# Every other weight chunk of the mixer split by a casting and an adding DMA, the chunks between on VectorE

## The chip, the cores and the metric

The kernel runs on one core of a Trainium2 chip. The metric is the device time of one execution in microseconds; of several runs the median is given.

## What is computed

One layer of a decoder with hybrid attention over 16 meta tokens and 512 tokens, model width 1024, all in float32. Of the reference, cut:

```python
h = concat(meta_tokens, x)
u = rmsnorm(h, attn_norm)
z = u @ w_in                # q, k, v of three attentions, an indexer, three gates
y_sb = stick_breaking(q_sb, k_sb, v_sb)                  # 4 heads
y_sp = indexed_sparse_attention(rmsnorm(q_sp), rmsnorm(k_sp), v_sp,
                                q_ix, k_ix, w_ix, rel_bias, top_k)   # 4 heads
y_df = rmsnorm(differential_attention(...))              # 4 heads of two maps
merged = (sigmoid(g_sb + b) * (y_sb @ w_br_sb) + sigmoid(g_sp + b) * (y_sp @ w_br_sp)
          + sigmoid(g_df + b) * (y_df @ w_br_df))
h = h + merged @ w_out
zf = rmsnorm(h, ffn_norm) @ w_up
h = h + (silu(causal_conv3(gate half of zf)) * (value half of zf)) @ w_down
return h[16:]
```

## The kernel before

All weights lie in memory as 133 chunks of 128x1024 float32 (512 KB), each eight 128x128 blocks. A float32 product is made of three passes of TensorE in a reduced type, fp32r: each operand is split into a high part (its value rounded to fp32r) and a low part (what is left), and `mm3` (L311) runs over the chunk's blocks three times: high part of the weights with the high part of the activations, high with low, low with high. So the low part `wl` of a chunk is first read in the third pass of its first half of the tokens (258 or 264 columns), after 16 matmuls of the chunk, and last in the third pass of its second half.

The chunks are used one after the other in the order of the list `order` (L279). First come the indexer's three, then those that PLAN (L46) names: units (`sb`, `sp`, `df`: three chunks each, q, k and v of two heads or one differential pair), gates (`g`: four chunks for half of a branch's gate) and branches (`b`: the output projection of an attention, half of it), then W_OUT, W_UP and W_DN, the last two being the feed-forward part. While dense chunks run on TensorE, the attentions of the units before run as streams: generators that `tick` moves on, one step after every eight matmuls of a chunk. They advance by clocks that the kernel books for each engine (`book`, L87); what a stream does next, and in which order the engines get the work, hangs on these booked costs.

A chunk is prepared by `prep` (L299): its raw float32 lands in a buffer `wr` by a DMA from SP's queue (L296), ACT casts it into `wh`, and `sub` (L108) subtracts, wl = wr - wh, on GpSimd (G, the profile's POOL) or VectorE (V, DVE), whichever would end earlier by the booked clocks (with 1 us in favour of GpSimd). There are three raw buffers, two of wh and two of wl. Each user of a chunk k (`dense`, `branch`, `up` and the like) calls `prep(k)` and `prep(after.get(k))`, so the next chunk is prepared while this one is multiplied, and its raw data is loaded another chunk ahead. A wl buffer is free once TensorE has ended the third pass of the chunk two before.

Names that come up below: `xh`, `xl` are the activations' parts, `psd` and `psw` the PSUM banks of dense chunks and of streams, `tmp` work tiles of the streams, `r` a reciprocal of a softmax sum, `m` and `work` the top-k search, `G` gates, `y` an attention's output, `pm` and `pt` transposed weights of attention, `qk` queries and keys, moved between partitions by DMAs of SP's queue (L632), `W` a bias tile that a DMA from POOL's queue (L122, `gdma`) loads. Operations that go through the booking helper all have line 99.

The low part is chosen and written here:

```python
    def sub(out, a, b, hv=HV):
        t = clock["P"]
        tv = max(clock["V"], t) + V.cost(out) + hv
        e = G if max(clock["G"], t) + G.cost(out) < tv else V
        e.tensor_tensor(out, a, b, OP.subtract)
```

Of the kernel before, what the change touches and what calls it, by code (L numbers as in the profile page):

```python
# [8 lines left out]
F32 = mybir.dt.float32  # L9
F32R = mybir.dt.float32r  # L10
AF = mybir.ActivationFunctionType
OP = mybir.AluOpType
# [3 lines left out]
P = 128  # L16
# [24 lines left out]
W_BR, W_OUT, W_UP, W_DN = 51, 59, 67, 111  # L41
# [14 lines left out]
def tile_kernel(ctx: ExitStack, tc, hT, wpk, par, bias, yT):  # L56
    nc = tc.nc
# [16 lines left out]
    HVW = 1000  # L74
    HV = 500

    def book(e, cost):
        c = cur[0]
        clock[e] = max(clock[e], clock["P"]) + cost
        c["t"] = max(clock[e], c["t"] + cost, clock["P"] + cost) + LAT  # L80

    class Timed:
# [11 lines left out]
        def __getattr__(self, op):  # L94
            f = getattr(self.eng, op)

            def run(out, *a, **k):
# [5 lines left out]
    V = Timed("V", nc.vector, 1.04, 150, scalar_tensor_tensor=(1.25, 105), tensor_tensor_scan=(2.16, 110),  # L103
              tensor_tensor_reduce=(1.0, 255), match_replace=(1.04, 220))
    S = Timed("S", nc.scalar, 0.84, 190)
    G = Timed("G", nc.gpsimd, 2.3, 200)
# [7 lines that stand above are left out]
# [6 lines left out]
    def gdma(out, x):  # L120
        book("G", 1050)
        nc.gpsimd.dma_start(out, x)  # L122
# [9 lines left out]
    wp = ctx.enter_context(tc.tile_pool(name="wp", bufs=2))  # L132
# [43 lines left out]
    def tmp(dt=F32):  # L176
        return ap_.tile([P, T], dt, tag="tmp", bufs=caps["tmp"], name="tmp")
# [99 lines left out]
    wraw, wsp = {}, {}  # L277
    plan = PLAN.split()
    order = [W_IX, W_QIX, W_QIX + 1]  # L279
# [10 lines left out]
    assert sorted(order) == list(range(NCHUNK))  # L290
    after = dict(zip(order, order[1:]))

    def load(k):
        if k is not None and k not in wraw:
            r = wp.tile([P, 8, P], F32, tag="raw", bufs=3, name=f"wr{k}")
            nc.sync.dma_start(r, wpk[k].rearrange("p (j c) -> p j c", c=P))  # L296
            wraw[k] = r

    def prep(k):  # L299
        if k is None or k in wsp:  # L300
            return
        load(k)
        r = wraw[k]
        wh = wp.tile([P, 8, P], F32R, tag="wh", bufs=2, name=f"wh{k}")
        wl = wp.tile([P, 8, P], F32R, tag="wl", bufs=2, name=f"wl{k}")
        S.copy(wh, r)
        sub(wl, r, wh, HVW)
        wsp[k] = (wh, wl)
        load(after.get(after.get(k)))

    def mm3(out, prs, xh, xl, start=True, stop=True):  # L311

# [19 lines left out]
    rs = const.tile([P, T], F32, name="rs")  # L332
    take("tmp", 10)
    for k in (W_IX, W_QIX):
        wraw[k] = wp.tile([P, 8, P], F32, tag="raw", bufs=3, name=f"wr{k}")
        wsp[k] = tuple(wp.tile([P, 8, P], F32R, tag=t, bufs=2, name=f"{t}{k}") for t in ("wh", "wl"))
    hs = [tmp() for _ in range(KT)]

    def load_h(*kts):
# [16 lines left out]
    nc.sync.dma_start(prm[:, C_QSP:], par[:, C_QSP:])  # L356
    load_h(6, 7)
    load(order[2])

    def wbank():  # L360
# [115 lines left out]
    def dense(k, evac, halves=HALQ, q0=Q0, into=(psd, psd)):  # L476
        prep(k)
        prep(after.get(k))
        for hf, (o, n) in enumerate(halves):
            d = into[hf]()  # L480
            s0 = q0 + o
            mm3(d[:, :n], [(k, j, j) for j in range(KT)], lambda kt: xh[:, kt, s0:s0 + n],
                lambda kt: xl[:, kt, s0:s0 + n])
            with tc.high_priority(offset=PRI):
                evac(hf, o, n, d[:, :n])
# [39 lines left out]
    for g in range(2):  # L525
        qh = tmp(F32R)
        ql = tmp(F32R)

        def ev_qix(hf, o, n, d):
            raw = tmp()  # L530
            V.tensor_tensor(raw[:, :n], d, rs[:, Q0 + o:Q0 + o + n], OP.mult)
            S.copy(qh[:, o:o + n], raw[:, :n])
            V.tensor_tensor(ql[:, o:o + n], raw[:, :n], qh[:, o:o + n], OP.subtract)

        if g:
            dense(W_QIX + g, ev_qix, into=(psd, wbank))
        else:
            prep(W_QIX + 1)
            for hf, (o, n) in enumerate(HALQ):
                ev_qix(hf, o, n, qixd[hf][:, :n])  # L540

        qd = [dram.tile([P, TQ], F32, name=f"qd{g}{e}") for e in range(2)]
        for d, x in zip(qd, (qh, ql)):
            nc.sync.dma_start(d, x[:, :TQ].bitcast(F32))
        for r, d in ((0, qd[0]), (32, qd[1]), (64, qd[0])):
            nc.sync.dma_start(qst[g][r:r + 32].bitcast(F32), d.rearrange("(j p) t -> p j t", p=32))
# [514 lines left out]
    for m in range(8):  # L1061
        a = gates[0, m // 4][:, m % 4]
# [12 lines left out]
    def ft(dt=F32):  # L1075
        return ffn.tile([P, TQ], dt, tag="ft", bufs=10, name="ft")

    for m in range(8):
        nc.sync.dma_start(hm[:, m], hT[:, m, Q0:])
        k = W_OUT + m  # L1080
# [53 lines left out]
    for f in range(NF):  # L1134
# [6 lines left out]
        c = ft()  # L1141
# [4 lines left out]
        a = ft()  # L1146
# [9 lines left out]
    for m in range(8):  # L1156
# [3 lines left out]
        for c in sorted({e // 8 for e in range(e0, e1)}):  # L1160
            k = W_DN + c
# [82 lines left out]
```

## Time and profile before

| | before |
|---|---|
| runs, us | 912.95, 916.18, 915.88 |
| median, us | 915.88 |
| profiled execution, us (its span) | 913.53 (911.6) |
| granted TensorE clock, mean | 0.99 |
| PE busy in the span | 873.7 us, 96% |
| DVE busy | 554.9 us, 61% |
| ACT busy | 452.9 us, 50% |
| POOL busy | 322.3 us, 35% |
| DMA from SP's queue / from POOL's | 91.30 MB / 2.42 MB |

The profile is of one execution. The span is the time from its first to its last instruction; the execution's own time lies 1.9 us above it. Busy shares are means over the whole span: the mixer lasts to about 487 us, W_OUT to about 535, the feed-forward part the rest.

### The profile page before, as it was taken

The page shows a single profiled execution, that of the slowest core. Times are in us where ns is not written, and L with a number is a line of the kernel's source. Part 1 is how long each engine was busy: PE and PEld are TensorE (multiplying, and loading weights), DVE is VectorE, ACT ScalarE, POOL GpSimd, SP SyncE. Part 2 cuts the span into 40 slices and gives each one's busy share as a digit, 9 for nine tenths or more (in the row PEclk, how much of TensorE's full clock was granted, in tenths as well). Part 3 has the DMA queues.
Part 4 walks back from the last instruction along what each step waited for, and adds up shares of the span by engine and source line. Part 5 has one row for each costly group of instructions (what it writes and reads, how often), then busy time and mean ns, then how long its engine had stood idle before and what let it go on. Part 6 is the DMA issues. An engine that isn't in the chain of part 4 may idle for free.

```text
span 911.6 us, 15425 instructions
## 1 busy us (share of the span) xinstructions
PE 873.7 (96%) x6066; PEld 810.0 (89%) x6066; DVE 554.9 (61%) x1125; ACT 452.9 (50%) x848; POOL 322.3 (35%) x195
## 2 busy tenths in 40 slices
PE   7998999898999999889998999999999999999998
PEld 6988989798999999779998999999999999888886
DVE  6579988877677888787437445555555555322221
ACT  7466877676756686735654343333333333211110
POOL 2534233332445425665353233344444344200100
PEclk9999999999999999999999999999999999999999
DMA  6585213441234522432233433232333332233330
GB/s 231 163 247 177 70 47 104 107 118 47 71 98 118 139 67 87 106 92 68 70 93 118 137 91 95 93 93 93 93 93 93 93 93 93 93 117 105 116 101 23
DMA packets 32359, 94.68 MB, mean 104 GB/s; under 512 B 4313, under 2 KB 4457, under 8 KB 32288
## 3 DMA queue, kind: packets, MB, share of 16 engines
q1 hardware_dynamic: 31568, 91.30, 33.8%
q0 software_dynamic: 720, 2.42, 1.0%
q8 instruction: 47, 0.77, 0.4%
q14 instruction: 24, 0.20, 0.1%
HBM read 80.88 MB, written 5.86 MB: 95 GB/s over the span
## 4 chain that ended last, share of the span: by engine, by line
PE 71%; DVE 15%; ACT 8%; issue 3%; DMA 2%; POOL 1%; SPq 0%; DVEq 0%; ACTq 0%; POOLq 0%
PE psd L183 49%; PE psw L183 21%; DVE tmp L99 7%; ACT tmp L99 3%; DVE work L99 3%; DVE m L99 1%; PE psw L187 1%; DVE G L99 1%; ACT wh L99 1%; DMA qk<-qk 1%; ACT G L99 1%; DMA tmp<-hT 1%; POOL wl L99 1%; DVE pt L99 1%; DVE r L99 1%
## 5 line engine op out<-in xcount | busy, mean ns | idle before, releaser
L99 POOL TENSOR_TENSOR wl<-wr,wh 128x1024 fp32r<-128x1024 f32 x79 | 193.0, 2443 | 333.1 <-ACT wh L99 241.0
L99 ACT CAST wh<-wr 128x1024 fp32r<-128x1024 f32 (+2 forms) x137 | 139.4, 1020 | 175.4 <-PE psd L183 117.6
L183 PE MATMUL psd<-xh,wh 128*128 128x258 f32 (+2 forms) x792 | 118.4, 289 | 1.8 <-DVE tmp L99 1.2
L183 PE MATMUL psd<-xl,wh 128*128 128x258 f32 (+2 forms) x792 | 119.0, 290 | 0.0
L183 PE MATMUL psd<-xh,wl 128*128 128x258 f32 (+2 forms) x792 | 117.9, 289 | 0.0
L99 DVE TENSOR_TENSOR wl<-wr,wh 128x1024 fp32r<-128x1024 f32 (+3 forms) x58 | 67.0, 1157 | 69.0 <-PE psd L183 60.6
L183 PEld LDWEIGHTS psd<-xh,wh 128*128 128x128 f32 x792 | 104.5, 191 | 3.4 <-ACT kst L99 1.0
L183 PEld LDWEIGHTS psd<-xl,wh 128*128 128x128 f32 x792 | 104.9, 191 | 1.0
L183 PEld LDWEIGHTS psd<-xh,wl 128*128 128x128 f32 x792 | 104.8, 191 | 0.7
L99 ACT ACTIVATE tmp<-tmp 128x264 f32<-128x264 f32 (+7 forms) x154 | 69.2, 474 | 16.8 <-DVE tmp L99 14.5
L99 POOL TENSOR_TENSOR ft<-ft 128x512 f32<-128x512 f32 x22 | 46.5, 2114 | 82.5 <-DVE ft L99 79.1
L99 DVE SCALAR_TENSOR_TENSOR ft<-ft,prm 128x512 f32<-128x512 f32 x44 | 58.4, 1328 | 20.4 <-ACT ft L99 19.6
L183 PE MATMUL psw<-uh,wh 128*128 128x256 f32 (+2 forms) x264 | 47.0, 320 | 0.0
L183 PE MATMUL psd<-ul,wh 128*128 128x258 f32 (+2 forms) x264 | 46.9, 319 | 0.0
L183 PE MATMUL psw<-ul,wh 128*128 128x256 f32 (+2 forms) x264 | 46.9, 319 | 0.0
L183 PE MATMUL psd<-uh,wl 128*128 128x258 f32 (+2 forms) x264 | 46.8, 319 | 0.0
L183 PE MATMUL psw<-uh,wl 128*128 128x256 f32 (+2 forms) x264 | 46.8, 319 | 0.0
L183 PE MATMUL psd<-uh,wh 128*128 128x258 f32 (+2 forms) x264 | 46.8, 319 | 0.0
L183 PE MATMUL psd<-ah,wl 128*128 128x512 f32 x176 | 45.8, 396 | 0.0
L183 PE MATMUL psd<-al,wh 128*128 128x512 f32 x176 | 45.8, 396 | 0.0
L183 PE MATMUL psd<-ah,wh 128*128 128x512 f32 x176 | 45.8, 396 | 0.0
L99 ACT CAST ah<-ft 128x512 fp32r<-128x512 f32 x22 | 13.7, 622 | 64.6 <-POOL ft L99 64.6
(193 smaller groups left out, 1653.7 us busy)
## 6 DMA issues: line engine op xcount, KB each, us to landing
wr<-wpk SPq DMA_DIRECT2D x131, 512.0 KB, 3.6
qk<-qk SPq DMA_DIRECT2D x48, 132.0 KB, 3.7
gd<-tab SPq DMA_DIRECT2D x8, 328.0 KB, 6.2
tmp<-hT SPq DMA_DIRECT2D x8, 264.0 KB, 5.9
W<-gd POOLq DMA_DIRECT2D x8, 264.0 KB, 3.6
qk<-tmp SPq DMA_DIRECT2D x16, 128.5 KB, 2.3
hm<-hT SPq DMA_DIRECT2D x8, 257.0 KB, 4.3
yT<-ft SPq DMA_DIRECT2D x8, 256.0 KB, 2.0
```

Source lines behind the costliest of these rows:

```text
L99: return f(out, *a, **k)
L183: PE.matmul(out, lhsT, rhs, **k)
L187: PE.transpose(out, x, ident[:x.shape[0], :x.shape[0]])
```

## The change

The 25 chunks at places 10, 12, ... 58 of `order` (all before W_OUT), the set `two`, get no raw load. A DMA from GpSimd's queue reads the float32 chunk and writes it, cast, into wh; ACT writes wl = -wh; a second DMA from GpSimd's queue (line 334 of the changed kernel) reads the chunk again and adds it to wl. The chunks between (places 9, 11, ... 57) are loaded and cast as before, and their low part is always written by VectorE. Both preparations are issued by the `prep` of the chunk between, so that of a chunk in `two` a chunk earlier than before. There are two raw buffers instead of three, and three of wh instead of two. `load` skips the chunks in `two`, and is called for the next chunk instead of the one after it. W_OUT, W_UP and W_DN keep their split by `sub`.

```diff
--- before.py
+++ after.py
@@ -290,23 +290,48 @@
     assert sorted(order) == list(range(NCHUNK))
     after = dict(zip(order, order[1:]))
 
+
+
+
+    two = set(order[10:order.index(W_OUT):2])
+
+    def chunk(k):
+        return wpk[k].rearrange("p (j c) -> p j c", c=P)
+
+    def parts_of(k):
+        wh = wp.tile([P, 8, P], F32R, tag="wh", bufs=3, name=f"wh{k}")
+        wl = wp.tile([P, 8, P], F32R, tag="wl", bufs=2, name=f"wl{k}")
+        wsp[k] = (wh, wl)
+        return wh, wl
+
     def load(k):
+        while k in two:
+            k = after.get(k)
         if k is not None and k not in wraw:
-            r = wp.tile([P, 8, P], F32, tag="raw", bufs=3, name=f"wr{k}")
-            nc.sync.dma_start(r, wpk[k].rearrange("p (j c) -> p j c", c=P))
+            r = wp.tile([P, 8, P], F32, tag="raw", bufs=2, name=f"wr{k}")
+            nc.sync.dma_start(r, chunk(k))
             wraw[k] = r
 
     def prep(k):
         if k is None or k in wsp:
             return
+        assert k not in two
         load(k)
         r = wraw[k]
-        wh = wp.tile([P, 8, P], F32R, tag="wh", bufs=2, name=f"wh{k}")
-        wl = wp.tile([P, 8, P], F32R, tag="wl", bufs=2, name=f"wl{k}")
+        wh, wl = parts_of(k)
         S.copy(wh, r)
-        sub(wl, r, wh, HVW)
-        wsp[k] = (wh, wl)
-        load(after.get(after.get(k)))
+        a = after.get(k)
+        if a in two:
+            V.tensor_tensor(wl, r, wh, OP.subtract)
+        else:
+            sub(wl, r, wh, HVW)
+        load(a)
+        if a in two:
+            wh, wl = parts_of(a)
+            gdma(wh, chunk(a))
+            S.activation(wl, wh, AF.Copy, scale=-1.0)
+            book("G", 1050)
+            nc.gpsimd.dma_start(wl, chunk(a), accum_op=OP.add)
 
     def mm3(out, prs, xh, xl, start=True, stop=True):
 
@@ -332,8 +357,8 @@
     rs = const.tile([P, T], F32, name="rs")
     take("tmp", 10)
     for k in (W_IX, W_QIX):
-        wraw[k] = wp.tile([P, 8, P], F32, tag="raw", bufs=3, name=f"wr{k}")
-        wsp[k] = tuple(wp.tile([P, 8, P], F32R, tag=t, bufs=2, name=f"{t}{k}") for t in ("wh", "wl"))
+        wraw[k] = wp.tile([P, 8, P], F32, tag="raw", bufs=2, name=f"wr{k}")
+        parts_of(k)
     hs = [tmp() for _ in range(KT)]
 
     def load_h(*kts):
```

The changed order on GpSimd's queue, at chunks 27 to 30 of the first plan entries (the number behind wl, wh or wr is the chunk's). Before:

```order
L99 TENSOR_TENSOR wl27_1079<-wr27_813,wh27_1078 128x1024
L99 TENSOR_TENSOR tmp_991<-tmp_808,qk_989 128x514
L99 TENSOR_TENSOR qk_1095<-tmp_948,qk_1093 128x528
L99 TENSOR_TENSOR wl28_1191<-wr28_953,wh28_1190 128x1024
L99 TENSOR_TENSOR wl29_1328<-wr29_1082,wh29_1327 128x1024
L99 TENSOR_TENSOR wl30_1422<-wr30_1194,wh30_1421 128x1024
```

After:

```order
L122 DMA wh28_1082<-wpk 128x1024
L99 TENSOR_TENSOR tmp_989<-tmp_806,qk_987 128x514
L99 TENSOR_TENSOR qk_1098<-tmp_946,qk_1096 128x528
L334 DMA wl28_1083<-wpk 128x1024
L122 DMA wh30_1324<-wpk 128x1024
L334 DMA wl30_1325<-wpk 128x1024
```

The four subtracts have left the queue. Chunks 28 and 30 have two DMA issues each in their place; those of 27 and 29 went to VectorE.

ACT's queue at chunk 28. Before:

```order
L99 ACTIVATE pmw2_450<-pmw2_450 2x16
L99 CAST wh28_1190<-wr28_953 128x1024
L99 ACTIVATE tmp_943<-tmp_943 128x144
L99 ACTIVATE tmp_946<-tmp_946 128x272
```

After:

```order
L99 ACTIVATE pmw2_448<-pmw2_448 2x16
L99 CAST wh29_1318<-wr29_1080 128x1024
L99 ACTIVATE wl28_1083<-wh28_1082 128x1024
L99 ACTIVATE tmp_941<-tmp_941 128x144
L99 ACTIVATE tmp_944<-tmp_944 128x272
```

The cast of chunk 29 has moved ahead to where that of chunk 28 stood, and the pass that writes -wh of chunk 28 follows it.

TensorE's queue at the start of the branch b2a, whose first chunk is 55: xh and wl are the last dense chunk before it, y the attention's output, ones and blk the sums of a head norm. Before:

```order
L183 MATMUL psw<-tmp,ones_81 128x256
L183 MATMUL psd<-xh,wl_4930 128x264 x8
L183 MATMUL psd<-y,wh_5028 128x258 x3
L183 MATMUL psd<-y,wh_5028 128x256 x3
L183 MATMUL psd<-y,wh_5028 128x258 x3
L183 MATMUL psw<-tmp,blk 128x264
L183 MATMUL psw<-qk 2x16 x2
L183 MATMUL psw<-qk 128x144 x2
L183 MATMUL psw<-qk 128x272 x2
L187 MATMUL psw<-ident,tmp 128x128 x4
L187 MATMUL psw<-ident,tmp 16x128
L183 MATMUL psd<-y,wh_5028 128x258 x4
```

After:

```order
L183 MATMUL psd<-y,wh_4969 128x258 x3
L183 MATMUL psd<-y,wh_4969 128x256 x3
L183 MATMUL psd<-y,wh_4969 128x258 x3
L183 MATMUL psw<-tmp,ones_81 128x258
L183 MATMUL psw<-tmp,blk 128x264
L183 MATMUL psw<-tmp,ones_81 128x256
L187 MATMUL psw<-ident,tmp 128x128 x4
L187 MATMUL psw<-ident,tmp 16x128
L183 MATMUL psw<-tmp,blk 128x264
L183 MATMUL psw<-qk 2x16
L183 MATMUL psw<-qk 128x144
L183 MATMUL psw<-qk 128x272
```

The ones matmuls of df3's head norm, which gives the y that the branch reads in its next matmuls, now stand behind the branch's first nine, and the stream matmuls that stood after them are fewer.

## Rows read from the trace of the kernel before

**Rows 1.** The stretches: span, busy time and instructions per engine, granted clock, DMA share, GB/s.

```profile
core 0: us, PE busy (x) PEld busy (x) DVE busy (x) ACT busy (x) POOL busy (x), PEclk, DMA share, GB/s
90.00:430.00 340.00, 319.77 (x2545) 309.82 (x2544) 274.16 (x689) 230.17 (x503) 145.78 (x90) 0.98 0.32 90
...
535.00:907.00 372.00, 372.00 (x2108) 323.81 (x2107) 161.39 (x186) 114.77 (x139) 103.31 (x46) 1.00 0.31 93
```

**Rows 2.** The chain of waits from 90 to 430 us, shares by line.

```profile
by line: PE psd L183 29.4%; DVE tmp L99 16.7%; PE psw L183 8.2%; ACT tmp L99 7.3%; issue 4.3%; DVE m L99 3.5%; DVE work L99 3.4%; ACT wh L99 2.6%; PE psw L187 2.6%; DMA qk<-qk 2.6%; ACT G L99 2.3%; DVE G L99 1.8%; POOL wl L99 1.6%; DVE pt L
```

**Rows 3.** PE's waits from 90 to 430 us: in total, times, longest.

```profile
PE psw L183 <- ACT tmp L99: 5.8, 4, 2.7
```

**Rows 4.** Groups, 90 to 430 us: shapes and count | busy us, mean ns | idle before.

```profile
L99 POOL TENSOR_TENSOR wl<-wr,wh 128x1024 fp32r<-128x1024 f32 x38 | 93.2, 2454 | 133.8 <-ACT wh L99 101.0 <-ACT tmp L99 19.6 <-PE psw L183 6.0
...
L99 DVE TENSOR_TENSOR wl<-wr,wh 128x1024 fp32r<-128x1024 f32 x3 | 3.7, 1218 | 0.0
...
L99 ACT CAST wh<-wr 128x1024 fp32r<-128x1024 f32 x40 | 41.7, 1042 | 18.7 <-PE psd L183 7.6 <-issue 6.0 <-POOL qk L99 5.0
...
L122 POOL DMA_DIRECT2D W<-gd x5 | 2.8, 555 | 21.0 <-DVE mx L99 16.5 <-PE psd L183 4.2 <-POOL tmp L99 0.3
```

**Rows 5.** Timeline: start us, duration us, engine, line, operation.

```profile
314.58 2.02 DVE L99 TENSOR_TENSOR r<-r,nlam 128x1 f32<-128x1 f32 x1
...
314.19 2.39 POOL L99 TENSOR_TENSOR wl<-wr,wh 128x1024 fp32r<-128x1024 f32 x1 [1.05 <-ACT wh L99]
```

**Rows 6.** DVE groups, 90 to 430 us, columns as in rows 4.

```profile
L99 DVE SCALAR_TENSOR_TENSOR tmp<-tmp 128x264 f32<-128x264 f32 x12 | 9.5, 791 | 0.1
...
L99 DVE TENSOR_TENSOR r<-r,nlam 128x1 f32<-128x1 f32 x16 | 8.3, 519 | 0.3
...
L99 DVE SCALAR_TENSOR_TENSOR tmp<-psw,tmp 128x264 f32<-128x264 f32 x12 | 5.1, 421 | 3.0 <-ACT tmp L99 2.9
...
L99 DVE RECIPROCAL r<-r 128x2 f32<-128x2 f32 x16 | 2.5, 155 | 2.7 <-ACT tmp L99 2.7
...
L99 DVE TENSOR_SCALAR work<-work 128x528 f32<-128x528 f32 x1 | 0.4, 424 | 0.0
```

**Rows 7.** The chain's pieces: start us, us, engine, tile, line.

```profile
123.22 2.28 DVE pmw L99
...
231.74 1.81 DVE r L99
...
342.34 1.91 DVE tmp L99
```

**Rows 8.** DMA issues of the whole execution: count, KB each, median us to landing.

```profile
wr<-wpk SPq DMA_DIRECT2D x131, 512.0 KB, 3.6
...
gd<-tab SPq DMA_DIRECT2D x8, 328.0 KB, 6.2
...
W<-gd POOLq DMA_DIRECT2D x8, 264.0 KB, 3.6
```

**Rows 9.** Timeline of PE: third passes of two dense chunks, and of branch chunks.

```profile
95.44 1.10 PE L183 MATMUL psd<-xh,wl 128*128 128x256 f32 x8
...
106.06 1.11 PE L183 MATMUL psd<-xh,wl 128*128 128x258 f32 x8
...
470.23 1.11 PE L183 MATMUL psd<-xh,wl 128*128 128x256 f32 x8
...
477.44 0.40 PE L183 MATMUL psd<-y,wl 128*128 128x258 f32 x2
```

**Rows 10.** Timeline of PE at the start of b2a; idle time before in brackets.

```profile
369.07 0.59 PE L183 MATMUL psw<-tmp,ones 128*128 128x256 f32 x2
...
372.56 0.71 PE L183 MATMUL psw<-tmp,blk 128*128 128x264 f32 x2 [0.77 <-ACT tmp L99]
...
373.96 0.17 PE L183 MATMUL psw<-qk 128*2 128x16 f32 x1 [0.69 <-DMA qk<-qk]
...
374.68 1.25 PE L183 MATMUL psw<-qk 128*2 128x16 f32 x5 [0.55 <-POOL tmp L99]
...
376.65 0.56 PE L183 MATMUL psd<-y,wh 128*128 128x258 f32 x1
```

## The prediction

> **What bounds the kernel now.** I read the stretches first [rows 1]. From 535 us on (W_UP, W_DN) TensorE is busy for all of its 372.0 us and the change splits none of those chunks: nothing to win. From 90 to 430 us, where the mixer's dense chunks run beside the attention streams, PE is busy 319.8 of 340.0 us. These 20.2 idle us (2.2% of the time) are about the ceiling of any gain. The granted clock is 0.98 there, the upper level (2.4 GHz) nearly throughout. VectorE is busy 274.2 us (81%), POOL 145.8 (43%).
>
> Next the chain by line in that stretch [rows 2]: the DVE lines tmp, m, work and G hold 16.7 + 3.5 + 3.4 + 1.8 = 25.4% of it, POOL's low parts only 1.6%. So POOL itself is late hardly anywhere. PE's waits agree: the largest, 5.8 us in 4 times, is for an ACT operation on tmp [rows 3].
>
> Then what makes DVE slow. POOL's subtract of a chunk's low part lasts 2.45 us, 38 of them [rows 4]. While one runs, a DVE operation that reads two SBUF operands ends only when POOL's ends [rows 5]: the 128x1 subtract into r lasts 2.02 us, to 316.60, beside a POOL subtract that ends at 314.19 + 2.39 = 316.58. A reciprocal of r, which reads one operand, takes 0.155 us, and the subtract averages 0.519 over its 16 instances; 128x264 with both operands in SBUF averages 0.791 us, with one in PSUM 0.421 [rows 6]. So the cost of POOL's subtracts is not their own 93.2 us but what they do to DVE.
>
> **The change, part by part.**
> *Removed: POOL's subtracts.* In the changed order 47 of POOL's 79 are gone; 7 stay at the mixer's start and 25 after its end, in W_OUT and W_UP. Six pieces of the chain are DVE operations locked so, of 1.81 to 2.28 us, 12.34 us together, three of which are shown [rows 7]. Free, I price three at 0.16 us (128x1 or 2x16) and three at 0.42 (the 128x264 row), 1.74 us together. That leaves 10.6 us of lock on the chain: **-10.6 us**. Bounds: nothing, where another stream's work fills the place of the locked operation, and 14.0, with a third of the (0.791 - 0.421) x 12 + (0.519 - 0.155) x 16 = 10.3 us that two groups alone lose off this list [rows 6].
>
> *Added: DVE subtracts.* The 25 chunks between get theirs on DVE for certain; 3 of the mixer's subtracts were there before, so it is 22 more. One takes 1.218 us [rows 4]: 22 x 1.22 = 26.8 us. Bounds: 0 (they fill DVE's idle 66 us) and 26.8 (all on the chain). A subtract falls at an arbitrary place of the chain, of which DVE holds 25.4% [rows 2]: **+6.8 us**.
>
> *Moved: the split of the other 25.* A casting DMA into wh, an ACT pass that writes wl = -wh, an adding DMA into wl. ACT's new pass stands for its cast (1.04 us [rows 4]): no cost. The 25 raw loads leave SP's 131 [rows 8], so that the two raw buffers left serve half as many chunks: no cost; without that halving a load of 3.6 us would stand before a cast. Wh has a third buffer, and the casting DMA is issued a chunk earlier than its chunk is needed: that chunk's 48 matmuls cover it, and without them its landing of 3.6 us or more would show. There are two reads of a chunk where there was one, with the 16 engines 32% busy [rows 1]: room. On POOL's queue, 50 issues at 0.555 us [rows 4] stand for 47 subtracts at 2.45: no cost.
>
> The adding DMA has a deadline. A chunk's wl buffer is free when PE has ended the third pass of the chunk two before it, at 95.44 + 1.10 = 96.54 in one case, and it is first read at 106.06 [rows 9]: 9.5 us. From this go ACT's 1.04 us, some 0.3 us between steps and the landing L. No row shows a casting or an adding DMA. Bounds: a plain chunk lands in 3.6 us [rows 8]; to read, add and write might take two of those, 7.2; the longest plain landing shown is 6.2. I take L = 5, in the lower half, since the issue from POOL (264 KB) lands in 3.6 too. Then the dense chunks have 9.5 - 1.3 - 5 = 3.2 us to spare. The last branch chunk is the tightest: 470.23 + 1.11 = 471.34 to 477.44, 6.1 us [rows 9], so 0.2 us short; with ACT's queue at the two branch chunks before it **+1 us**. It decides at L = 8.2 in the dense part and at 4.8 at the last chunk.
>
> *The order at b2a's start.* Before, the second ones matmul of df3's head norm stands ahead of the third pass of a dense chunk. From it, at 369.07, to the first use of y at 376.65 it is 7.6 us, and PE idles 0.77 + 0.69 + 0.55 = 2.0 us in them [rows 10]. After, both ones matmuls stand behind nine y matmuls of the branch, and only transposes, blk and three qk matmuls, some 1.7 us, cover the norm until y is read again. Bounds: 0 (the norm's chain runs faster without locks) and 7.6 - 1.7 = 5.9. The middle, less a little lock: **+2.5 us**.
>
> **Sum.** -10.6 + 6.8 + 1 + 2.5 = -0.3 us. The rows come from an execution of 913.53 us (span 911.6), 2.35 below the median of the runs, 915.88. So 913.2 by the execution, and by the median **915.6 us**. A measurement of this kernel can tell about 0.5%, 4.6 us, from no change, so 911.3 to 920.5 is "same", and the forecast's own range.
>
> **Two rules of the Trainium skill speak against the split.** First the row: the 1024-element subtract takes 1218 ns on DVE, over one nanosecond an element, and only single operations run faster, as the 528 elements in 424 ns [rows 6]. The skill's page "SBUF — State Buffer", section "SBUF: two separate sides", warns that descriptors of a DMA issued from GpSimd's queue can't be written while DVE runs an operation in its 2-port mode. By that rule each of the 50 issues could start late behind such an operation, which is a rival below; no delay of this sort is seen at the POOL issues that land in 3.6 us. Second: the page "Collectives: The Full Stack", section "The bandwidth ceiling: the fold count and why AG ≠ RS ≠ AR", says that an add in the DMA needs two source reads. By it L would be near 7.2, 2.4 us late at each of the last three chunks, and the sum +6 instead of -0.3; no row here shows an adding DMA.
>
> **Rivals.**
> *Faster.* The locks go and DVE's subtracts fall into its idle time: -10.6, none of the 6.8 and half of the 3.5: -8.9, **907**; with its bounds 902 (-14.0) to 911. For it: DVE has 66 us idle, and the subtracts can start some 8 us ahead of need (9.5 - 1.04). Against: PE's waits are spread, and the largest ends on ACT, not on DVE [rows 3].
> *Slower: the adding DMA lands late.* From L = 8.2 on the dense chunks wait. At 9, half of the 22 dense ones 0.8 us each (9) and the last three 4.2, 2 and 1: +16, **932**. For it: no price in the trace, and three steps in a row (DMA, ACT, DMA) where there were two. Against: transfers of 264 to 512 KB land in 3.6 [rows 8].
> *Slower: POOL's queue starves.* Issues wait for DVE: 50, each 0.4 us late (half of a 0.8 us operation [rows 6]), a third of it seen: +7, **923**. Against it: few DVE operations here are as fast as the 424 ns one. The rule of the Trainium skill's page "SBUF — State Buffer", above, would do this.
> *It doesn't do what it says.* Streams advance by booked costs, and the bookings moved with the subtracts. If work gathers at b2a's start as far as its bound (5.9 for 2.5), and at two more starts by 2.5 each: +8, **924**.
>
> **How the numbers follow.** The forecast 0.36; faster 0.36; the adding DMA late 0.15; POOL's queue 0.05; streams moved 0.08. That makes faster 0.36, same 0.36, slower 0.28. Between equals the sum, at -0.3, decides for no change. The range goes from 902, the faster case's bound, to 930, which leaves the late case at L near 9 outside: with what lies under 902 and over 930, 2 in 10.
>
> **What would show it.** In the changed profile r's subtract (519 ns) and 128x264 (791 ns) should fall towards 0.16 and 0.42 us; if they don't, locks were not POOL's. Wl on DVE: 25 rows of about 1.22 us. The rows of DMA issues give L, and PE's waits name DMA wl if it lands late: over 6 us in all and the forecast is wrong. PE's idle time from 90 to 430 us should stay near 20 us; 12 or less is the faster case. A gap of over 5 us before the first y matmuls of b2a would be the moved norm; work gathered elsewhere shows as a new gap at a branch's start.

## The result and the profile after

The changed kernel takes 906.0 us (median; its runs 902.8 to 909.3) against 915.3 in the runs of the kernel before beside it: a ratio of 0.9896 with a 95% interval of 0.9875 to 0.9917. That is faster by 1.0%, beyond the 0.5% up to which the prediction speaks of no change. The time lies in the range (902 to 930), but not in the likeliest case (no change, 915.6). It is the first rival, faster, 902 to 911.

The profiled execution has a span of 904.7 us. The stretches of the changed kernel, columns as in [rows 1]:

```profile
90.00:430.00 340.00, 326.82 (x2643) 318.52 (x2642) 270.87 (x733) 239.53 (x521) 87.30 (x97) 0.99 0.54 127
...
535.00:900.00 365.00, 365.00 (x2058) 317.25 (x2057) 148.09 (x179) 109.96 (x129) 101.89 (x45) 1.00 0.31 95
```

From 90 to 430 us PE idles 13.2 us where it idled 20.2. VectorE is busy 270.9 us against 274.2 although it runs 25.6 us of subtracts where it ran 3.7, POOL 87.3 against 145.8. W_UP is untouched: it starts at 527.0 us, before at 534.0, and these 7.0 us are the whole difference of the spans (911.6 and 904.7).

The groups that answer to [rows 4, 6], of the changed kernel, 90 to 430 us (VectorE's in the first fence, POOL's in the second):

```profile
L99 DVE TENSOR_TENSOR wl<-wr,wh 128x1024 fp32r<-128x1024 f32 x21 | 25.6, 1217 | 0.0
...
L99 DVE SCALAR_TENSOR_TENSOR tmp<-tmp 128x264 f32<-128x264 f32 x12 | 5.7, 479 | 0.1
...
L99 DVE TENSOR_TENSOR r<-r,nlam 128x1 f32<-128x1 f32 x16 | 2.4, 154 | 0.3
```

```profile
L334 POOL DMA_DIRECT2D wl<-wpk x21 | 18.6, 884 | 91.4 <-ACT wl L99 69.3 <-ACT tmp L99 10.9 <-DVE mx L99 5.9
L122 POOL DMA_DIRECT2D wh<-wpk x22 | 12.4, 564 | 41.9 <-PE psd L183 35.0 <-PE psw L183 3.9 <-PE psw L187 2.9
```

These locks are gone: r's subtract takes 154 ns (519 before), 128x264 with two SBUF operands 479 (791). Over the whole execution VectorE without its subtracts of weights is busy 534.1 - 93.2 = 440.9 us, before 554.9 - 67.0 = 487.9. So 47 us went with GpSimd's subtracts; below, e14, which keeps the order of the kernel before, has 46.5 us less.

The chain by line, 90 to 430 us [rows 2], has VectorE's tmp at 10.5% (16.7% before), r no longer among the first, and the subtracts that VectorE now runs at 2.0%, which is 6.8 us:

```profile
by line: PE psd L183 44.4%; DVE tmp L99 10.5%; PE psw L183 10.1%; ACT tmp L99 4.4%; PE psw L187 3.8%; issue 3.4%; POOL tmp L99 2.3%; DVE wl L99 2.0%; DVE work L99 1.9%; DMA qk<-qk 1.8%; ACT wl L99 1.7%; DVE m L99 1.6%; DVE G L99 1.6%; POOL 
```

The DMA issues, as in [rows 8], give the landing times that were missing: 4.0 us for a casting DMA, 5.7 for an adding one (L was taken as 5).

```profile
wr<-wpk SPq DMA_DIRECT2D x106, 512.0 KB, 3.6
wh<-wpk POOLq DMA_DIRECT2D x25, 512.0 KB, 4.0
wl<-wpk POOLq DMA_DIRECT2D x25, 512.0 KB, 5.7
```

**Where the time came from, and where some of it went.** Dense chunks come in the same order in both kernels, so the end of a third pass (of the chunk's first half) can be set side by side. The streams' work between them is not the same, so the differences are a map, not a sum.

| the pass that ended, before, at | after, at | ahead by |
|---|---|---|
| 25.3 us | 26.4 | -1.2 |
| 32.0 | 38.2 | -6.2 |
| 156.4 | 159.2 | -2.8 |
| 230.2 | 218.5 | +11.7 |
| 370.6 (last before b2a) | 359.9 | +10.7 |
| 422.6 (first after b2b) | 415.4 | +7.2 |
| 534.0 (start of W_UP) | 527.0 | +7.0 |

So about 5 us are lost at 26 to 38 us, some 18 are won from 38 to 230 us, and 3.5 are lost again at b2a. The middle part, with about the same chunks in both, takes 114.7 us before (from 130.3) and 98.5 after (from 135.5). In them PE waits 9.1 us before, 7.5 of them for ACT's tmp and VectorE's pm, among locked operations as in [rows 7], and 1.1 us after; and the granted clock, which falls after such waits, is 0.97 before and 1.00 after. The row of the stretch before, then of the changed kernel:

```profile
130.30:245.00 114.70, 103.94 (x822) 100.67 (x820) 89.98 (x226) 83.54 (x175) 39.51 (x22) 0.97 0.31 86
```

```profile
135.50:234.00 98.50, 97.37 (x798) 95.25 (x797) 82.42 (x219) 78.11 (x162) 18.92 (x22) 1.00 0.58 135
```

In the changed kernel all of PE's waits from 90 to 430 us are 13.0 us, before 20.1, and 5.1 of them are a single one at b2a:

```profile
PE psw L183 <- DMA qk<-qk: 5.1, 1, 5.1
PE psw L183 <- DVE tmp L99: 3.4, 4, 1.7
PE psw L183 <- ACT tmp L99: 2.8, 2, 2.3
...
PE psd L183 <- DMA wl<-wpk: 0.2, 1, 0.2
```

The bad start, in the timeline of the changed kernel (start us, us, engine, line, operation):

```profile
29.48 2.34 POOL L99 TENSOR_TENSOR wl<-wr,wh 128x1024 fp32r<-128x1024 f32 x1 [2.63 <-ACT tmp L99]
29.51 2.61 DVE L99 TENSOR_TENSOR kst<-tmp 32x264 fp32r<-32x264 f32 x1 [1.34 <-ACT tmp L99]
...
32.72 0.55 PE L183 MATMUL psd<-xh,wh 128*128 128x258 f32 x1 [3.47 <-DVE tmp L99]
```

VectorE's subtract into kst, 32x264, starts 0.03 us after one of the seven subtracts left on GpSimd, and lasts 2.61 us. The evacuation of a PSUM bank stands behind it, and PE waits 3.47 us. After that PE runs at the lower level (1.2 GHz) for a while: the granted clock of the first 38 us is 0.92, before 1.00, and a pass of eight matmuls takes 1.92 us instead of 1.11:

```profile
0.00:38.00 38.00, 27.30 (x172) 26.40 (x172) 24.72 (x57) 24.09 (x48) 11.15 (x26) 0.92 0.58 187
```

At b2a [rows 10], the changed kernel's PE idles 2.35 + 0.93 + 5.05 = 8.3 us, before 2.0:

```profile
363.52 0.70 PE L183 MATMUL psw<-tmp,ones 128*128 128x258 f32 x2 [2.35 <-ACT tmp L99]
364.06 0.71 PE L183 MATMUL psw<-tmp,blk 128*128 128x264 f32 x2
364.60 0.60 PE L183 MATMUL psw<-tmp,ones 128*128 128x256 f32 x2
365.04 0.71 PE L187 MATMUL psw<-ident,tmp 128*128 128x128 f32 x5
366.68 0.71 PE L183 MATMUL psw<-tmp,blk 128*128 128x264 f32 x2 [0.93 <-DVE tmp L99]
372.44 0.82 PE L183 MATMUL psw<-qk 128*2 128x16 f32 x3 [5.05 <-DMA qk<-qk]
```

### The profile page after: what moved, and what is told of

Same layout as the page of the kernel before. It is cut to its first block, busy times and chain, and to the rows that moved or that the text cites. A ratio compares the mean times of both kernels' runs of the same rounds, so it can differ in the third digit from the quotient of the medians.

```text
span 904.7 us, 15408 instructions
## 1 busy us (share of the span) xinstructions
PE 869.8 (96%) x6066; PEld 808.5 (89%) x6066; DVE 534.1 (59%) x1145; ACT 453.6 (50%) x848; POOL 248.9 (28%) x200
## 4 chain that ended last, share of the span: by engine, by line
PE 76%; DVE 10%; ACT 4%; DMA 4%; POOL 2%; issue 2%; SPq 0%; ACTq 0%; POOLq 0%; DVEq 0%
PE psd L183 53%; PE psw L183 21%; DVE tmp L99 4%; ACT tmp L99 2%; PE psw L187 2%; DMA wr<-wpk 2%; DMA qk<-qk 1%; DVE work L99 1%; DVE G L99 1%; ACT wl L99 1%; POOL tmp L99 1%; DVE wl L99 1%; DMA wh<-wpk 1%; DVE m L99 1%; DMA wl<-wpk 1%
## 5 line engine op out<-in xcount | busy, mean ns | idle before, releaser
L99 ACT CAST wh<-wr 128x1024 fp32r<-128x1024 f32 (+2 forms) x112 | 114.2, 1021 | 219.3 <-DMA wr<-wpk 171.9
L99 DVE TENSOR_TENSOR wl<-wr,wh 128x1024 fp32r<-128x1024 f32 (+2 forms) x80 | 93.2, 1166 | 70.1 <-PE psd L183 67.9
L99 POOL TENSOR_TENSOR wl<-wr,wh 128x1024 fp32r<-128x1024 f32 x32 | 81.1, 2537 | 180.1 <-PE psd L183 95.0
L99 ACT ACTIVATE tmp<-tmp 128x528 f32<-128x528 f32 (+7 forms) x154 | 69.0, 475 | 15.8 <-DVE tmp L99 13.4
L99 DVE SCALAR_TENSOR_TENSOR ft<-ft,prm 128x512 f32<-128x512 f32 x44 | 48.3, 1097 | 29.3 <-ACT ft L99 28.5
L334 POOL DMA_DIRECT2D wl<-wpk x25 | 22.1, 885 | 120.2 <-ACT wl L99 94.2
```

What stands on the lines that cost most here:

```text
L99: return f(out, *a, **k)
L334: nc.gpsimd.dma_start(wl, chunk(a), accum_op=OP.add)
```

## The experiments

Theories, after the result. **Locks** (a lock is a VectorE operation that ends only when GpSimd's does): GpSimd's subtracts cost what they do to VectorE, and a subtract on VectorE costs next to nothing. **Split**: the DMA split makes the gain. **Plan**: the streams' order, which follows the booked costs, makes it. Ratios are to runs of the kernel before beside each, with 95% intervals. The last column is VectorE's busy time without the subtracts of weights, a measure of the locks.

| kernel | ratio | median us | VectorE without wl, us |
|---|---|---|---|
| before | 1 | 915.3 | 487.9 |
| changed | 0.9896 (0.9875 to 0.9917) | 906.0 | 440.9 |
| e14_engine: plan of before, 47 subtracts on VectorE | 0.9856 (0.9842 to 0.9870) | 902.7 | 441.4 |
| e1_dve_all: the same, booked on VectorE | 0.9892 (0.9879 to 0.9905) | 905.1 | 441.8 |
| e2_dve_odd: every other one on VectorE | 0.9922 (0.9909 to 0.9936) | 907.4 | 464.3 |
| e3_split_only: split, the others on GpSimd | 0.9851 (0.9838 to 0.9864) | 901.3 | 465.0 |
| e4_odd_on_pool: plan of changed, the others on GpSimd | 0.9980 (0.9965 to 0.9995) | 912.0 | 470.9 |
| e11_unbooked | 0.9839 (0.9826 to 0.9852) | 900.1 | 445.2 |
| e12_start | 0.9857 (0.9842 to 0.9873) | 902.3 | 435.2 |
| e13_both | 0.9839 (0.9824 to 0.9854) | 901.1 | 436.6 |
| e8b_start | 0.9871 (0.9844 to 0.9897) | 902.7 | 442.6 |
| e9_all_dma | 1.0037 (1.0012 to 1.0061) | 919.8 | 450.2 |
| e6_bufs | 0.9994 (0.9982 to 1.0005) | 914.7 | 489.0 |
| e15_engine_all | 0.9851 (0.9828 to 0.9874) | 901.9 | 435.0 |

**The engine alone.** The cleanest of the tests leaves the plan of the kernel before as it is and changes only which engine executes the subtract, in a copy of `sub` that `prep` calls with the chunk's number:

```diff
         e = G if max(clock["G"], t) + G.cost(out) < tv else V
-        e.tensor_tensor(out, a, b, OP.subtract)
+        if e is G and 9 <= order.index(k) < order.index(W_OUT):
+            book("G", G.cost(out))
+            nc.vector.tensor_tensor(out, a, b, OP.subtract)
+        else:
+            e.tensor_tensor(out, a, b, OP.subtract)
```

> The kernel before with its booked costs, hence its plan, kept: every mixer subtract from place 9 on that it gave to GpSimd is still booked there but run by VectorE (47 of them, 57 us). No split by DMA, buffers as before. If the locks are what GpSimd's subtracts cost and a VectorE subtract finds room: -11 to -14, 901 to 904 us. If a VectorE subtract costs a quarter of its time: -12 + 14, 917 us. If the order of the streams made the gain of the change: 915 us.

It took 902.7 us, the figure of the locks. VectorE has 47 subtracts more, of 1266 ns (59.5 us), and is busy 568.0 us in all instead of 554.9; still the kernel is 1.4% faster. PE idles 11.6 us from 90 to 430 us, and the locked rows are at their free values:

```profile
90.00:430.00 340.00, 328.40 (x2621) 319.23 (x2621) 288.49 (x746) 236.07 (x512) 61.19 (x52) 0.98 0.32 91
```

```profile
L122 DVE TENSOR_TENSOR wl<-wr,wh 128x1024 fp32r<-128x1024 f32 x40 | 51.0, 1276 | 3.9 <-ACT wh L99 3.8
...
L99 DVE SCALAR_TENSOR_TENSOR tmp<-tmp 128x264 f32<-128x264 f32 x12 | 5.2, 436 | 0.1
...
L99 DVE TENSOR_TENSOR r<-r,nlam 128x1 f32<-128x1 f32 x16 | 2.3, 151 | 0.2
```

So the engine alone is worth some 13 us: that is what the locks cost, less what the subtracts cost on VectorE. The run gives only this net. The chain of the same profile has the subtracts on it (DVE wl), 2.3% or 7.8 us, so it doesn't say that they are free:

```profile
by line: PE psd L194 42.0%; PE psw L194 10.7%; issue 10.5%; DVE tmp L99 7.5%; PE psw L198 3.4%; ACT tmp L99 2.9%; DMA qk<-qk 2.8%; DVE work L99 2.4%; DVE wl L122 2.3%; DVE m L99 2.0%; DVE G L99 1.6%; POOL qk L99 1.5%; POOL tmp L99 1.2%; POO
```

The split by DMA has no part in this kernel.

**Both halves of the change, and all on VectorE.** In the kernel before, the subtract of places 9 on (e1), or of every other one (e2), is given to VectorE and booked there; in the changed kernel the others go back to `sub` (e3):

```diff
+        if k in mixer:            # e2: if k in odd
+            V.tensor_tensor(wl, r, wh, OP.subtract)
+        else:
+            sub(wl, r, wh, HVW)
```

```diff
-        if a in two:
-            V.tensor_tensor(wl, r, wh, OP.subtract)
-        else:
-            sub(wl, r, wh, HVW)
+        sub(wl, r, wh, HVW)
```

> The kernel before (its buffers, its loads, no split by DMA), with the low parts of all 50 mixer chunks from place 9 on taken by VectorE: 47 more subtracts there, 57 us, and none on GpSimd beside them. If the locks were the price and a VectorE subtract finds room in VectorE's idle time: about 904 us, r's subtract near 0.155 us. If a VectorE subtract costs its chain share (25%): -12 + 14 = about 917 us. If the gain came from the split by DMA: 915 us or more.

> The kernel before, with the low parts of the 25 chunks at places 9, 11, ... 57 taken by VectorE; the chunks at 10, 12, ... are split as before, on GpSimd. This is one half of the change alone. If locks are the price: half of them gone, -5 to -6, and 22 more VectorE subtracts: 910 us if they are free, 916 if each costs a quarter. If the split by DMA made the gain: 915 us.

> The changed kernel, but the chunks between are given to sub as before, which puts 24 of the 25 on GpSimd. The other half of the change alone. If locks are the price: half of them are back, 906 + 5 = 911 us, r's subtract at about 0.33 us. If the split by DMA made the gain: 906 us, or some us less since VectorE is free of 24 subtracts (29 us, a quarter of it 7): 899 us.

e1, at 905.1, is near the locks' figure without the split. Against e14, with the same subtracts on VectorE, it is 0.0036 (3.3 us) slower by the booking alone. e2 and e3 each have half of the lock time back (464 and 465 us in the table). e2 gains 7.3 us, near half of e14's gain and a little over the 5 expected. e3 did not do what the locks alone say (911): it is among the fastest, although r's subtract is at 407 ns again. It differs from the changed kernel in engine and in booking, so the next run parts the two.

**Plan of the changed kernel, engine of e3.** The 25 subtracts run on GpSimd but are booked on VectorE:

```diff
-            V.tensor_tensor(wl, r, wh, OP.subtract)
+            book("V", V.cost(wl))
+            nc.gpsimd.tensor_tensor(wl, r, wh, OP.subtract)
```

> The changed kernel with the 25 subtracts of the chunks between run by GpSimd but still booked on VectorE, so that the streams advance as in the changed kernel. If locks are the price: half of them are back with nothing else changed: 910 to 913 us, r's subtract at about 0.33 us. If the order of the streams made the gain: 906 us. If VectorE's subtracts cost a quarter of their time: 7 less on that account.

It takes 912.0: at the changed kernel's plan, GpSimd in place of VectorE costs 6 us (7.7 by the ratios), which is the locks' figure (r, at 157 ns, happens to be spared in this order; VectorE's lock time in all is 30 us up on the changed kernel's). But against e3, with the same engines but for one subtract, it is 10.7 us slower. Not all of that is the booking: in their profiles the order at the start is the same on every engine (compared up to 36 us), yet PE waits 4.6 us there in e4 and 1.2 in e3, and e4 is 3.9 us behind at the end of the next pass (37.0 against 33.1). That leaves some 7 us to the plan, as far as one profile of each tells. So the plan is worth about as much as the locks, and the locks' share can be read only where the plan is held: e14 against before, and e4 against the changed kernel.

**What the booking costs the changed kernel.** Same engines, but the 25 subtracts are not booked on VectorE's clock:

```diff
-            V.tensor_tensor(wl, r, wh, OP.subtract)
+            nc.vector.tensor_tensor(wl, r, wh, OP.subtract)
```

> The changed kernel with the same instructions on the same engines, but the 25 subtracts of VectorE are not booked on VectorE's clock, so that the streams don't give way to them in the plan. In the built order the two ones matmuls of df3's head norm then stand ahead of the first nine y matmuls of b2a again. If the 9.2 us that PE idles at b2a's start come from this booked cost: 5 or more of them go, 900 us. If VectorE's real work delays df3: the gap stays, 906 us or more.

900.1 us, the first theory's number, but not shown to be its cause. Its b2a keeps 0.85 + 3.41 us of waits, of the changed kernel's 8.3:

```profile
357.03 0.71 PE L183 MATMUL psw<-tmp,blk 128*128 128x264 f32 x2 [0.85 <-DVE tmp L99]
357.38 0.37 PE L183 MATMUL psw<-qk 128*2 128x16 f32 x1
361.16 1.18 PE L183 MATMUL psw<-qk 128*2 128x16 f32 x8 [3.41 <-DMA qk<-qk]
```

But its start has no long wait in the profiled execution (1.1 us), though the order up to 36 us is the changed kernel's on every engine. The pass that ends at 38.2 us there ends at 32.8 here, 5.4 us ahead, and the last such pass of the mixer at 458.7 instead of 464.3, 5.6 ahead. So between these two profiles the gain is all made at the start, and what e11 wins at b2a is lost again behind it.

**The start.** First the raw data: the chunk at place 3 gets a tile of the gates, so that the next load comes earlier (a first reading of the start blamed ACT's cast, which waits 2.77 us for it). Then the lock: the 7 subtracts at places 2 to 8 run on VectorE with their booking kept (as in e14, for `order.index(k) < 9`).

```diff
+            if k == order[3]:
+                r = ap_.tile([P, 4, TQ], F32, tag="G", bufs=4, name=f"wr{k}")
...
+        if k == order[2]:
+            load(order[4])
```

> The changed kernel with a third place for raw weights at the start alone: the raw data of the chunk at place 3 goes to a tile that the gates use later, so that the raw data of the chunk at place 4 is loaded earlier. In the changed kernel ACT's cast of that chunk waits 2.77 us for the load, the evacuations queued behind it are late, and PE waits 3.5 us at 29 us, after which the granted clock is at its lower level until 38 us. If the missing third raw buffer makes this start: 906 - 2.5 - 2.5 = 901 us, with 0.8 to 1.2 us idle there. If the place where GpSimd's subtract meets the evacuation's subtract on VectorE decides (a lock, by chance of some tens of ns): the wait may stay, 906 us.

> The changed kernel with its booked costs kept, and the 7 low parts at the mixer's start (places 2 to 8), which GpSimd writes, run by VectorE. If the changed kernel's bad start (3.5 us of idle PE at 29 us, then the lower clock) is a lock of VectorE by GpSimd's subtract: the start has about 1 us idle and clock 1.00, 906 - 5 = 901 us, and the runs lie closer together. If it is the load of the raw data: no change, 906.

In e8b's profiled execution the cast no longer waits, yet PE waits 5.5 us at the same place, and its runs go from 899.6 to 907.6: the raw data is not the cause, or not alone. The subtract on GpSimd comes earlier there (26.68 to 29.03 us), and an operation on rs beside it takes 1.65 us. With the subtracts off GpSimd (e12) the long wait is gone, the clock of the first 38 us is 1.00, and the runs lie between 901.6 and 903.0. So the start is the lock. Part of the gain is lost later: from 38 to 90 us e12's clock is 0.93, the changed kernel's 1.00. How near it is shows in e3, whose start has the same order as the changed kernel's: there the first kst begins 0.05 us ahead of GpSimd's subtract, and lasts 0.42 us.

```profile
28.96 0.42 DVE L99 TENSOR_TENSOR kst<-tmp 32x264 fp32r<-32x264 f32 x1 [1.26 <-ACT tmp L99]
29.01 2.61 POOL L99 TENSOR_TENSOR wl<-wr,wh 128x1024 fp32r<-128x1024 f32 x1 [2.63 <-ACT tmp L99]
```

**Both repairs.** e13 has e11's and e12's edits.

> The changed kernel with both repairs: VectorE's 25 subtracts not booked (900.1 us alone), and the 7 at the start run by VectorE but booked on GpSimd. If both costs are real and separate: 897 to 900 us; the start's share is smaller than alone, since the profiled run without booking had only 1.1 us idle there.

901.1 us, at e11's ratio: the start's repair adds nothing on top. The profile shows where it goes. e13 is 4.0 us ahead of e11 at the end of one pass (71.1 against 75.1 us) and 2.0 behind at the next (80.9 against 78.9). Between them PE waits 2.17 us for an evacuation that stands behind a subtract on VectorE, and runs at a granted clock of 0.58 from 74 to 82 us (e11: 1.00):

```profile
73.34 1.20 DVE L336 TENSOR_TENSOR wl<-wr,wh 128x1024 fp32r<-128x1024 f32 x1
...
74.81 0.76 DVE L99 TENSOR_TENSOR tmp<-psd,rs 128x264 f32<-128x264 f32 x2
...
75.28 2.13 PE L194 MATMUL psd<-xh,wh 128*128 128x264 f32 x8 [2.17 <-DVE tmp L99]
```

e12 and e15 have the same wait (2.17 and 2.15 us). Here a subtract on VectorE is not free: VectorE is busy for 7.97 of the 8 us from 72 on, and an earlier start only makes PE wait for it. From e12 to e13, booking is worth 0.0018 of the time (1.6 us), within the two intervals; what it is worth alone stays open.

**All 50 chunks by DMA.**

```diff
-    two = set(order[10:order.index(W_OUT):2])
+    two = set(order[9:order.index(W_OUT)])
...
+        if k in two:
+            cast(k)
+            wh, wl = wsp[k]
+            S.activation(wl, wh, AF.Copy, scale=-1.0)
+            book("G", 1050)
+            nc.gpsimd.dma_start(wl, chunk(k), accum_op=OP.add)
...
+        a = after.get(k)
+        load(a)
+        cast(a)
```

> The changed kernel with all 50 mixer chunks from place 9 on split by casting and adding DMA, none by VectorE or GpSimd; the casting DMA of a chunk is issued one chunk ahead. If VectorE's 25 subtracts cost some us and the locks are gone in either case: 3 to 7 us below the changed kernel, 899 to 903. If the adding DMA's landing (5.7 us at 25 of them) grows with twice as many: PE waits for DMA wl at many chunks, 910 us or more.

919.8 us: the changed kernel's gain is gone (ratio to the kernel before 1.0037; runs from 911 to 924 us). An adding DMA lands in 5.8 us, hardly longer than with 25 of them, so the landing did not grow; but PE now waits for it, and more for the moves of qk:

```profile
PE psw L183 <- DMA qk<-qk: 8.8, 4, 5.0
PE psd L183 <- DMA wl<-wpk: 7.4, 7, 2.2
```

Whether its casts or its adds come too late was not parted.

**Two raw buffers.** In the kernel before, with the load one chunk ahead:

```diff
-            r = wp.tile([P, 8, P], F32, tag="raw", bufs=3, name=f"wr{k}")
+            r = wp.tile([P, 8, P], F32, tag="raw", bufs=2, name=f"wr{k}")
...
-        load(after.get(after.get(k)))
+        load(after.get(k))
```

> The kernel before with two raw buffers in place of three and the raw data loaded one chunk ahead, not two; nothing else is changed. The prediction says that two raw buffers cost nothing only because half of the chunks need none. With all chunks in them: if a raw load of 3.6 us then stands before each cast, some of the 50 mixer chunks wait, 920 us or more; if the loads are hidden anyway, 915 us.

914.7 us, no difference. The term was right at nothing, but not for its reason: the loads are hidden with all chunks in two buffers.

**The last candidate.** e14 with the first seven subtracts on VectorE as well.

> As the run that keeps the plan of the kernel before and has VectorE run GpSimd's mixer subtracts (902.7 us), with the 7 at places 2 to 8 on VectorE too: no subtract of a weight is on GpSimd before W_OUT. If the locks at the start cost as much here as in the changed kernel (about 4 us): 899 us. If they meet nothing that PE waits for, as the idle 0.8 us there says: 902 us, no difference.

901.9 us, no difference from e14. In that plan these seven meet nothing that PE waits for at the start (0.8 us in e14); what is won up to 73 us (2.7 us) is lost at the wait at 76 us told above. The fastest kernels, e11, e13, e3, e15, e14 and e12, have intervals that overlap, 1.4 to 1.6% under the kernel before, and each beats the changed one by its median; e14 needs neither the second read of 25 chunks nor a third wh buffer.

## Why the prediction was right or wrong

The range held because it reached down to the faster rival's bound, and the mechanism was named; the forecast itself, no change, was the wrong one of two cases with equal chances, which the sum decided.

**Removed: -10.6 us (bounds 0 and -14). This step was mis-sized.** Right in kind: r's subtract went from 519 to 154 ns (0.16 was the price), 128x264 from 791 to 479 (0.42), and the waits of 130 to 245 us, where four of the six locked pieces stood, fell from 9.1 to 1.1 us. But "Six pieces of the chain are DVE operations locked so" left seven out. Four of them in the chain of the kernel before, and the last as the timeline has it, beside the subtract that ends at 245.88 + 2.54 = 248.42:

```profile
105.28 2.78 DVE tmp L99
...
149.71 1.91 DVE tmp L99
...
218.90 2.10 DVE tmp L99
...
246.77 2.21 DVE tmp L99
```

```profile
245.88 2.54 POOL L99 TENSOR_TENSOR wl<-wr,wh 128x1024 fp32r<-128x1024 f32 x1 [6.56 <-ACT wh L99]
246.69 2.28 DVE L99 SCALAR_TENSOR_TENSOR tmp<-tmp,gsub 128x514 f32<-128x514 f32 x1
```

The 13 operations on the chain from 90 to 430 us that begin beside a subtract of GpSimd's and end up to 0.6 us after it last 25.5 us; the same operations take 5.7 us in e14. So the lock on the chain is 19.9 us, nearly twice the term and beyond its bound.

**Added: +6.8 us.** Each subtract was priced at a quarter of its time, the chain's share of VectorE. In the changed kernel's chain the subtracts stand for 2.0% of 340 us, 6.8 us, so by this measure the term came out. The bound of 0 did not: no run shows them free, and one of them holds up PE in e13. In e14 the measure gives 7.8 us of 51.0, less than a quarter. What a run shows is only the net: with 47 subtracts moved and the order held, -13.2 us. By the prediction's prices that would be -10.6 + 47 x 1.22 x 0.254 = +4.0 us; by the chain it is -19.9 + 7.8 = -12.1. So the two terms together had the wrong sign for e14, and the chain puts that on the locks. How the net divides no run shows by itself. That VectorE looked full (81% busy) was no bar, since 46.5 us of lock left it for the 59.5 us of subtracts that came. And from 90 to 430 us the chain holds 19.9 of the some 33 us of lock, but 7.8 of the 51.0 us of subtracts, which are prepared ahead of their use.

**Moved: the split, +1 us.** L is 5.7 us, taken 5, and the bound of 7.2 held. As said, only the last chunks come short: PE waits for DMA wl 0.8 us in 2 times up to 490 us, the longer being 0.58 at the last branch chunk.

```profile
471.15 0.51 PE L183 MATMUL psd<-y,wl 128*128 128x258 f32 x2 [0.58 <-DMA wl<-wpk]
```

The split has no gain of its own that these runs can tell: e13, with it, and e14, without it, are within their intervals. On the Trainium skill's rule (its page "Collectives: The Full Stack", section "The bandwidth ceiling: the fold count and why AG ≠ RS ≠ AR": an add needs two source reads), the trace agrees in direction: 5.7 us against 4.0 for the cast, not twice. The Trainium skill's other rule (its page "SBUF — State Buffer", section "SBUF: two separate sides": descriptors of a DMA issued from GpSimd's queue can't be written while VectorE runs an operation in its 2-port mode) did not show: the issues take 0.56 (cast) and 0.88 us (add) on POOL, and W's DMA lands in 3.9 us (3.6 before).

**b2a: +2.5 us.** Idle time there went from 2.0 to 8.3 us, 6.3 more where the bound was 5.9. But the kernel before also waited 2.6 us on G later in the same branch, and this wait is gone after; from the last pass before b2a to the first after b2b the changed kernel loses 3.5 us. So the gap was undersized and its net cost was near, in part by luck: the wait on G had no place in the prediction.

**Not in the sum: the start.** The seven subtracts left on GpSimd were named but given no price. One of them locks an evacuation there, and with the lower clock after it this costs 3.6 us (0.0039 of the time, e12 against the changed kernel). "It doesn't do what it says" came true in part: work gathered at b2a beyond its bound; the start's gap is a lock, not moved work.

With the chain's sizes and the start in it, the sum reads -19.9 + 6.8 + 0.8 + 3.5 + 3.6 = -5.2 us, an estimate from the rows above; the two profiled spans differ by -6.9, and the medians by -9.3, with an interval of -11.4 to -7.6. So some of it stays unexplained.

## What to carry to other kernels

Price an operation on another engine by what runs beside it: 47 subtracts of 2.4 us on GpSimd that hardly anybody waited for cost 46.5 us of VectorE's time in locks, and moving them to the engine they disturbed made the kernel 13 us faster, though that engine looked full and got 59.5 us of work for it. Count every locked operation on the chain: six were priced here, 13 stood there. Look for such locks in groups of small operations whose mean is well above that of a like one with a PSUM operand or with one operand. Where a plan is made from booked costs, change the engine with the booking held, and the booking by itself: here booking alone moved the time by 3 us (e14 to e1) and, less the luck of the start, by some 7 (e3 to e4).

## What the runs showed that I had not expected

The locks seen here have GpSimd first: the same subtract into kst took 0.42 us when it began 0.05 us ahead of GpSimd's, and 2.61 us when it began 0.03 us behind. In e11 and e9, too, it took 0.42 us, beginning 0.21 and 0.23 us ahead. By such a difference, in one and the same order of instructions, the start of a profiled execution is 5 us longer or not, and a short wait of PE is paid a second time in the clock (0.92 in the first 38 us). The changed kernel's four runs have spans of 900.7, 903.1, 904.7 and 907.2 us at granted clocks of 0.994, 0.992, 0.991 and 0.987; only the one of 904.7 was profiled, so that the others differ by their start is likely, not shown. It also means that runs whose start holds this near meeting (the changed kernel, e3, e4, e9, e11) are compared with a chance of some us between them. And the adding DMA is cheap by itself, 5.7 us for 512 KB, 1.7 more than the casting one.
